# Four kinds of small transfers moved to ScalarE's DMA queue, with a new stage order and new buffer counts, in a hybrid decoder block

## The chip, the cores and the metric

One core of one Trainium2 chip runs the whole kernel. The metric is the device time of one execution in microseconds (us), lower is better; the kernel before is given by the median of three runs. The core has five engines, each of which runs its own list of instructions in order: TensorE (PE in the profile), VectorE (DVE), ScalarE (ACT), GpSimd (POOL) and SyncE (SP). An instruction that has to wait holds up everything behind it on its own engine. A DMA is started by an instruction on an engine's list (here on SP's, and after the change on ACT's too) and carried out by 16 DMA engines.

## The reference

The reference is one decoder layer over 2048 tokens of width 1024, in float32: two groups of heads side by side (gated DeltaNet and retention), an output projection, and a gated MLP with a causal convolution. Cut to what matters:

```python
n    = rms_norm(x, attn_norm_w)                       # (2048, 1024)
proj = n @ w_in                                       # q,k,v,gate,a,b | q,k,v,gate
# gated DeltaNet group: 4 heads of 128; q,k,v = silu(causal conv of width 4)
g    = -exp(a_log) * softplus(a + dt_bias);  beta = sigmoid(b)
gcum = cumsum(g, inside a chunk);  decay = exp(where(causal, gcum_i - gcum_j, -inf))
m    = where(strict, (k * beta) @ k.T * decay, 0)
T    = inverse(eye + m)                               # unit lower triangular
u_base, w_mat, qk = T @ (v * beta), T @ (k * beta * exp(gcum)), (q @ k.T) * decay
for each chunk:                                       # carries state (128 x 128) per head
    u     = u_base - w_mat @ state
    o     = (q * exp(gcum)) @ state + qk @ u
    state = state * exp(gcum_last) + (k * exp(gcum_last - gcum)).T @ u
o_gdn = rms(o) * norm_w * silu(gate)
# retention group: 4 heads of 128, rotary on q,k, fixed decay gamma per head
for each chunk:
    o = ((q @ k.T) * d_mat) @ v + (q * xi) @ r;   r = r * gamma**C + (k * zeta).T @ v
o_ret = silu(gate) * rms(o)
h  = x + concat(o_gdn, o_ret) @ w_out
gg, uu = split(causal_conv_width3(rms_norm(h, mlp_norm_w) @ w_up))   # 2 x 2816
out = rms_norm(h + (silu(gg) * uu) @ w_down, final_norm_w)
```

## The kernel before

**Three stages.** The mixers (up to about 1207 us of the span) run over 4 blocks of 512 tokens, `b = 0..3`. Then `mlp_up` makes the two MLP inputs (to about 2090 us), and `mlp_down` the output. Almost all the work is matmuls on PE. A float32 product is made of three matmuls on float32r halves (high by high, high by low, low by high): L111 to L113 where weights are the stationary side, L383 to L385 where the tokens are. The kernel uses a Strassen-like scheme of 7 products for the output projection and the MLP, whose adds run on DVE.

**Stages of a block.** Each token of `ORDER` is a block number and a stage name. `pro` is the first norm; `k0`, `q0`, `kq`, `v0` are the retention projections (`tok` matmuls). `dec` is `decays`: from the decay inputs it makes the decay sums `gps` (two small matmuls, L460 and L461), transposes them (`gct`, L475) and writes them to device memory as `gdr` (L479). `a0`..`a3` are four steps of one DeltaNet head: `dmat` (L481 to L491) reads `gdr` back as a broadcast to all 128 partitions into `D` (L485) and takes its exponential on ACT (L491); `gdn_kq` and `gdn_v` make q, k, v (`chm` matmuls, convolution, transposes) and the triangular matrix `N`; `gdn_z` (L580 to L587) writes the four diagonal 32-blocks of `N` to `z1` in device memory, by four DMAs. `b0`, `b1` are `gdn_base` for two heads at a time: it reads `z1` back and inverts the 32-blocks on POOL (L600 to L607).

**The recurrence.** `g0`, `g1` are the two pairs of DeltaNet heads: first `gdn_lvls` builds the full inverse from its blocks (`yps`, `ttps`), then four steps of `gdn_rec`, one for each chunk of 128 tokens. One step is a chain that goes back and forth between PE and DVE: `ks` (L679, state times q and k) on PE, a subtraction on DVE (L682), `wps` (L690) on PE, a scaling on DVE (L694), `sps` (L698) on PE, the state's update on DVE (L700), and from there the next step's `ks`. I call each way from PE over DVE back to PE a link; a step has three.

**The rest of a block.** `h0`..`h3` are retention heads (`ret_head`): `rr` (L778), transposes `rtr` (L788), `rkk` (L794), and `ro` (L801 and L802). `p0`, `p1` are the gates. `G0`, `G1` transpose the gated outputs (`mxt`, L420). `W1`..`W7` are the products of the output projection (`wo`, with the split of its input on ACT at L872). `N` is `norm2`: it transposes the normalized rows (`nps`, L907) and writes them to device memory as `n2d` (L909), where `mlp_up` reads them.

**What sets the order.** `ORDER` fixes in which order the stages are handed to the framework. The framework then schedules by a simulation of the engines, with `ORDER` as the priority, and writes a fixed list for each engine. So a token's place moves its instructions, but other stages' instructions come between them. `BUFS` and constants like `NUU` (the buffers of the split inputs in `mlp_down`) set how many buffers each name has, and with that how far one stage may run ahead of another. All DMAs are on SP, so that a DMA that waits for its data holds up all loads behind it.

Of the kernel before, what the change touches and what calls it, by code (L numbers as in the profile page):

```python
# [15 lines left out]
NW = 5  # L16
LA = 1
NHH = 3
NUU = 8
NVR = 4  # L20
NVV = 20
NWUR = 2
# [11 lines left out]
NLATE = 4  # L34
NXR = 7
FD = 4
BUFS = {"n1": 8, "ykq": 5, "kv": 5, "NT": 5, "AT": 5, "o": 2, "n2s": 10, "xk": 2, "og": 1, "co": 7, "Cw": 4,
        "wx": 1, "wsq": 3, "wvr": 3, "wvt": 7, "ca": 8, "mix": 6, "D": 8, "rk": 5, "rq": 4, "rv": 7, "Ar": 1,
        "Nb": 6, "rot": 1, "rrow": 7}

ORDER = ("0pro 0k0 0v0 0dec 0a0 0q0 0a1 0h1 0a2 0b0 0h0 0a3 0b1 0g0 0kq 0p1 0p0 0h3 0h2 0g1 1pro 1k0 0G0 "
# [5 lines left out]
P = 128  # L47
S = 2048
D = 1024
# [3 lines left out]
NT = TB // P  # L53
# [13 lines left out]
def unit(pool, tag, shape, dt=F32, **kw):  # L67

    n = int(np.prod(shape[1:]))
    t = pool.tile([P, U1], dt, tag=tag, name=tag, **kw)[:, :n]  # L70
    if len(shape) == 3:
        t = t.rearrange("p (a b) -> p a b", a=shape[1])
    elif len(shape) == 4:
        t = t.rearrange("p (a b c) -> p a b c", a=shape[1], b=shape[2])
    return t
# [3 lines left out]
def hybrid_block(ctx, tc, x, xT, w_kq, w_v, w_g, w_rk, w_r0, w_r, w_o, w_u, w_d, cols, rows, fnr, masks, rot, out):  # L79
# [47 lines left out]
    seq = []  # L127
    for name in ORDER.split():
        seq += [(None, None, None)] if name == "U" else items[int(name[0])][name[1:]]
# [73 lines left out]
def mixers(ctx, tc, base, base_used, marks, drp, mm3, gamma, mhalf, n1w, n2w, gcw, gv127, epsr, gnw, n2d, hd,  # L203
           x, xT, w_kq, w_v, w_g, w_rk, w_r0, w_r, w_o, rows, masks, rot):
    nc = tc.nc
# [93 lines left out]
    def al(tag, shape, dt=F32):  # L299
        return unit(ap_, tag, shape, dt, **({"bufs": BUFS[tag]} if tag in BUFS else {}))  # L300

    def half(owner, key, tag, i):

        if key not in owner:
            owner[key] = al(tag, [P, 2, TB])
        return owner[key][:, i]
# [32 lines left out]
    def A_items(b, st):  # L339
# [90 lines left out]
        def decays(_):  # L430
            ab = st["ab"]
            a = ab[:, :, 0]
# [43 lines left out]
            gt = small("gt", P, 1)[:16]  # L476
            DVE.tensor_copy(gt, ps[:16, :P])
            gd_ = st["gdr"] = drp.tile([NH, NT, P], F32, tag="gdr", name="gdr")
            nc.sync.dma_start(gd_.rearrange("h c b -> (h c) b"), gt)  # L479

        def dmat(h):  # L481
            def f(_):
                gc = st["gc"]
                Dm = st["D", h] = half(st, ("Dp", h // 2), "D", h % 2).rearrange("p (a b) -> p a b", a=NT)
                nc.sync.dma_start(Dm.rearrange("p a b -> p (a b)"),  # L485
                                  st["gdr"][h].rearrange("a b -> (a b)").partition_broadcast(P))
                for c in range(NT):
                    j = c * NH + h
                    DVE.scalar_tensor_tensor(Dm[:, c, :], Dm[:, c, :], gc[:, j:j + 1], below,
                                             op0=ALU.subtract, op1=ALU.min)  # L490
                ACT.activation(Dm, Dm, AF.Exp)  # L491
            return f
# [83 lines left out]
        v4 = lambda t: t.rearrange("p (c d) -> p c d", d=P)  # L576
# [3 lines left out]
        def gdn_z(h):  # L580
            def f(_):
                if ("z1", h // 2) not in st:
                    st["z1", h // 2] = drp.tile([2, NT, 4, 32, 32], F32, tag="z1", name="z1")
                z1 = st["z1", h // 2][h % 2]
                for k in range(4):
                    sl = slice(k * 32, (k + 1) * 32)
                    nc.sync.dma_start(z1[:, k].rearrange("c j i -> j c i"), v4(st["hd", h]["N"])[sl, :, sl])  # L587
            return f


# [251 lines left out]
    def W_items(b):  # L842
# [19 lines left out]
        def product(i):  # L862
            def f(_):
                vs = [load_v(tc, ap_, w_o, i, k, {"vr": ("wvr", BUFS["wvr"]), "vt": ("wvt", BUFS["wvt"]), "v": ("wv", NWV)},
                             wvc, drp) for k in range(NH)]
# [34 lines left out]
        def norm2(_):  # L900
            for kk in range(4):
                ns = al("n2s", [P, 2, TB])
                for i in range(2):
                    k = 2 * kk + i
                    ps = mbank("nps")
                    for m in range(NT):
                        PE.transpose(ps[:, m * P:(m + 1) * P], C[m][:, k * P:(k + 1) * P], ident)  # L907
                    ACT.activation(ns[:, i], ps, AF.Copy, scale=n2w[:, k:k + 1])
                marks["n", b, kk] = nc.sync.dma_start(n2d[b, kk].rearrange("k p t -> p k t"), ns)  # L909
        return {f"W{i}": [(None, None, product(i))] for i in ORD_DN} | {"N": [(None, None, norm2)]}  # L910

    sts = [dict() for _ in range(NB)]
# [185 lines left out]
def mlp_down(ctx, tc, marks, mm3, sfa, mhalf, hd, aud, w_d, fnr, out):  # L1098
# [15 lines left out]
    def load_u(i, tp):  # L1114
# [8 lines left out]
        for c in range(2):  # L1123
            us.append(unit(wq, "uu", [P, 8, P], F32R, bufs=NUU))
        u3 = unit(wq, "u3", [P, 2, NP - 8, P], F32R, bufs=2)
# [153 lines left out]
```

## Time and profile before

| | before |
|---|---|
| median of 3 runs | 2513.75 us (2513.45 to 2514.49) |
| the profiled execution's own time | 2519.11 us |
| its span in the trace | 2517.3 us |
| VectorE (DVE) busy | 1627.8 us, 65% of the span |
| ScalarE (ACT) busy | 1000.4 us, 40% |
| GpSimd (POOL) busy | 581.7 us, 23% |

The trace is of one execution; its own time is 1.8 us longer than its span. "Busy" leaves out the time an engine takes to start DMAs. In the views, a row `A <- B` says that the engine's instruction A was idle until instruction B on another engine was done.

### The profile page before, as it was taken

The page shows a single profiled execution, that of the slowest core. Times are in us where ns is not written, and L with a number is a line of the kernel's source. Part 1 is how long each engine was busy: PE and PEld are TensorE (multiplying, and loading weights), DVE is VectorE, ACT ScalarE, POOL GpSimd, SP SyncE. Part 2 cuts the span into 40 slices and gives each one's busy share as a digit, 9 for nine tenths or more (in the row PEclk, how much of TensorE's full clock was granted, in tenths as well). Part 3 has the DMA queues.
Part 4 walks back from the last instruction along what each step waited for, and adds up shares of the span by engine and source line. Part 5 has one row for each costly group of instructions (what it writes and reads, how often), then busy time and mean ns, then how long its engine had stood idle before and what let it go on. Part 6 is the DMA issues. An engine that isn't in the chain of part 4 may idle for free.

```text
span 2517.3 us, 35733 instructions
## 1 busy us (share of the span) xinstructions
PE 2430.2 (97%) x12476; PEld 2036.1 (81%) x12476; DVE 1627.8 (65%) x3198; ACT 1000.4 (40%) x2150; POOL 581.7 (23%) x891
## 2 busy tenths in 40 slices
PE   8999799999999989998899999999999999999998
PEld 7877688787888878887688888888888888888887
DVE  5755677435652663445889898897565567555795
ACT  6634445434433542324454443442222224433332
POOL 1355136531064205150011000000000001422180
PEclk9999799999999999999999999999999999999999
DMA  8756388863685646652889877867676868764794
GB/s 320 245 190 218 115 319 318 306 222 136 229 285 161 212 159 212 247 186 85 319 340 351 316 296 286 306 254 273 241 251 224 285 240 283 221 211 152 240 300 135
DMA packets 285604, 609.64 MB, mean 242 GB/s; under 512 B 40880, under 2 KB 120944, under 8 KB 285424
## 3 DMA queue, kind: packets, MB, share of 16 engines
q1 hardware_dynamic: 285424, 607.36, 68.7%
q8 instruction: 98, 1.61, 0.3%
q14 instruction: 82, 0.67, 0.1%
HBM read 410.56 MB, written 196.71 MB: 241 GB/s over the span
## 4 chain that ended last, share of the span: by engine, by line
PE 79%; POOL 7%; DVE 6%; DMA 3%; ACT 3%; issue 2%; SPq 0%; POOLq 0%; DVEq 0%; ACTq 0%
PE p L111 10%; PE p L112 10%; PE p L113 10%; PE tok L383 5%; PE tok L385 5%; PE tok L384 5%; PE d L113 5%; PE d L112 5%; PE d L111 5%; POOL pers L605 2%; POOL pers L603 2%; PE chm L111 2%; PE chm L113 2%; PE chm L112 2%; PE wo L111 2%
## 5 line engine op out<-in xcount | busy, mean ns | idle before, releaser
L111 PE MATMUL p<-x,wu 128*128 128x512 f32 x1176 | 454.6, 391 | 6.2 <-ACT x L928 5.8
L112 PE MATMUL p<-x,wu 128*128 128x512 f32 x1176 | 458.5, 390 | 1.9 <-DVE x L929 1.9
L113 PE MATMUL p<-x,wu 128*128 128x512 f32 x1176 | 451.5, 390 | 0.0
L383 PE MATMUL tok<-wc,n 128*128 128x512 f32 (+2 forms) x768 | 274.0, 363 | 13.0 <-ACT n L371 9.6
L384 PE MATMUL tok<-wc,n 128*128 128x512 f32 (+2 forms) x768 | 276.1, 360 | 0.0
L385 PE MATMUL tok<-wc,n 128*128 128x512 f32 (+2 forms) x768 | 275.8, 362 | 0.0
L111 PEld LDWEIGHTS p<-x,wu 128*128 128x128 f32 x1176 | 221.2, 188 | 54.6 <-ACT x L928 8.3
L112 PEld LDWEIGHTS p<-x,wu 128*128 128x128 f32 x1176 | 221.0, 188 | 48.9 <-DVE x L929 3.2
L113 PEld LDWEIGHTS p<-x,wu 128*128 128x128 f32 x1176 | 221.0, 188 | 45.8
L1049 DVE SCALAR_TENSOR_TENSOR acc<-uc,base,acc 128x1023 f32<-128x1023 f32 (+1 forms) x176 | 221.3, 1280 | 41.3 <-ACT acc L1046 39.8
L1007 DVE TENSOR_TENSOR uc<-p,uc 128x512 f32<-128x512 f32 x224 | 153.6, 689 | 138.0 <-PE p L113 137.4
L177 POOL TENSOR_TENSOR vt<-vr 128x512 f32<-128x512 f32 x44 | 70.0, 1596 | 618.4 <-DMA au<-acc 422.9
L112 PE MATMUL d<-v,uu 128*128 128x512 f32 x448 | 174.3, 389 | 0.0
L111 PE MATMUL d<-v,uu 128*128 128x512 f32 x448 | 174.3, 389 | 0.0
L113 PE MATMUL d<-v,uu 128*128 128x512 f32 x448 | 174.3, 389 | 0.0
L383 PEld LDWEIGHTS tok<-wc,n 128*128 128x128 f32 x768 | 146.2, 191 | 32.8 <-ACT n L371 9.6
L384 PEld LDWEIGHTS tok<-wc,n 128*128 128x128 f32 x768 | 146.4, 191 | 19.6
L385 PEld LDWEIGHTS tok<-wc,n 128*128 128x128 f32 x768 | 145.4, 190 | 20.0
L111 PE MATMUL chm<-n,wc 128*128 128x512 f32 x384 | 152.9, 398 | 0.0
L113 PE MATMUL chm<-n,wc 128*128 128x512 f32 x384 | 152.2, 396 | 0.0
L112 PE MATMUL chm<-n,wc 128*128 128x512 f32 x384 | 152.0, 396 | 0.0
L1054 POOL COPY base<-uc 128x2 f32<-128x2 f32 x44 | 35.2, 799 | 454.4 <-DVE uc L1007 453.6
(247 smaller groups left out, 4897.0 us busy)
## 6 DMA issues: line engine op xcount, KB each, us to landing
wu<-wu SPq DMA_DIRECT2D x308, 512.0 KB, 6.0
wc<-wd SPq DMA_DIRECT2D x166, 512.0 KB, 5.5
wv<-wo SPq DMA_DIRECT2D x84, 512.0 KB, 5.9
wd<-wc SPq DMA_DIRECT2D x60, 512.0 KB, 5.1
ur<-au SPq DMA_DIRECT2D x56, 512.0 KB, 5.8
wur<-in_w_u SPq DMA_DIRECT2D x44, 512.0 KB, 6.1
au<-st SPq DMA_DIRECT2D x88, 256.0 KB, 4.6
vr<-in_w_d SPq DMA_DIRECT2D x44, 512.0 KB, 6.0
```

The source lines that it names most:

```text
L111: PE.matmul(ps, ah, bh, start=(first and i == 0), stop=False, skip_group_check=chk)
L112: PE.matmul(ps, ah, bl, start=False, stop=False, skip_group_check=chk)
L113: PE.matmul(ps, al, bh, start=False, stop=(i == n - 1), skip_group_check=chk)
L177: POOL.tensor_tensor(tt[:, j], a, b_, op=ALU.subtract)
L383: PE.matmul(ps, ah, wh, start=(k == 0), stop=False)
L384: PE.matmul(ps, ah, wl, start=False, stop=False)
L385: PE.matmul(ps, al_, wh, start=False, stop=(k == KT - 1))
L603: POOL.tensor_tensor(tm[:, :, :n], Nb[:, j:j + 1, j + 1:].to_broadcast([P, 8, n]), X[:, :, j:j + 1].to_broadcast([P, 8, n]), op=ALU.mult)
L605: POOL.tensor_tensor(X[:, :, j + 1:], X[:, :, j + 1:], tm[:, :, :n], op=ALU.add)
L1007: add = lambda o, ps, a: DVE.tensor_tensor(o, ps, a, op=ALU.add)
L1049: DVE.scalar_tensor_tensor(acc[:, t:], u[:, :T2 - t], w, acc[:, t:], op0=ALU.mult, op1=ALU.add)
L1054: POOL.tensor_copy(mhalo[:, ci], u[:, T2 - 2:])
```

## The change

Four lines change the engine that starts a DMA from SP to ACT: the write of the decay sums `gdr` (L479, 4 DMAs in the program), their broadcast to `D` (L485, 16), the blocks of the triangular matrices to `z1` (L587, 64) and the normalized rows to `n2d` (L909, 16), 100 DMAs together. The reads of `z1` and `n2d` stay on SP. Seven buffer counts change by one or two, and `ORDER` is rewritten in places.

```diff
@@ -16,7 +16,7 @@
 NW = 5
 LA = 1
 NHH = 3
-NUU = 8
+NUU = 10
 NVR = 4
 NVV = 20
 NWUR = 2
@@ -34,15 +34,15 @@
 NLATE = 4
 NXR = 7
 FD = 4
-BUFS = {"n1": 8, "ykq": 5, "kv": 5, "NT": 5, "AT": 5, "o": 2, "n2s": 10, "xk": 2, "og": 1, "co": 7, "Cw": 4,
-        "wx": 1, "wsq": 3, "wvr": 3, "wvt": 7, "ca": 8, "mix": 6, "D": 8, "rk": 5, "rq": 4, "rv": 7, "Ar": 1,
+BUFS = {"n1": 8, "ykq": 5, "kv": 4, "NT": 5, "AT": 6, "o": 2, "n2s": 11, "xk": 2, "og": 1, "co": 6, "Cw": 4,
+        "wx": 1, "wsq": 3, "wvr": 3, "wvt": 8, "ca": 8, "mix": 6, "D": 8, "rk": 5, "rq": 4, "rv": 8, "Ar": 1,
         "Nb": 6, "rot": 1, "rrow": 7}
 
-ORDER = ("0pro 0k0 0v0 0dec 0a0 0q0 0a1 0h1 0a2 0b0 0h0 0a3 0b1 0g0 0kq 0p1 0p0 0h3 0h2 0g1 1pro 1k0 0G0 "
-         "1dec 0G1 0W1 0W2 1q0 0W6 1a0 0W7 1a1 0W5 1a3 1v0 0W3 1h1 1b0 0W4 1a2 1h0 0N 1kq 1b1 1g0 2pro "
-         "1p0 1p1 1h2 1g1 1h3 2k0 1G0 1G1 2v0 2dec 1W1 1W2 2a0 1W6 2a1 1W7 1W5 1W3 2a2 2b0 2q0 1W4 2h1 "
-         "2a3 2b1 2h0 2g0 2g1 1N 3pro 2p1 2p0 2kq 2h2 2G0 3k0 2h3 2G1 3dec 2W1 2W2 3a1 3a0 2W6 3v0 3b0 "
-         "3q0 3h1 2W7 2W5 2W3 3h0 3a3 3p0 3a2 3b1 3g0 3kq 3h2 3h3 2W4 3g1 3G0 2N 3p1 3G1 3W1 3W2 3W6 3W7 "
+ORDER = ("0pro 0k0 0v0 0dec 0a0 0q0 0a1 0a2 0h0 0b0 0h1 0a3 0b1 0g0 0kq 0g1 0h2 0p1 1pro 0p0 1k0 0G0 0h3 "
+         "1dec 0G1 0W1 1a0 0W2 1q0 0W6 0W7 1a1 0W5 1a3 1v0 0W3 1h1 1b0 0W4 1a2 1h0 0N 1kq 1b1 1g0 2pro "
+         "1p1 1h2 1p0 1g1 1h3 2k0 1G0 1G1 2v0 2dec 1W1 1W2 2a0 1W6 1W7 1W5 1W3 2a2 2a1 2b0 2q0 1W4 2h1 "
+         "2a3 2b1 2h0 2g0 2g1 1N 3pro 2p1 2kq 2h2 2p0 2G0 3k0 2h3 2G1 3dec 3a0 2W1 2W2 3a1 2W6 3v0 3b0 "
+         "3q0 3h1 2W7 2W5 3a2 2W3 3h0 3a3 3b1 3kq 3p0 3g0 3h2 2W4 3g1 3G0 2N 3p1 3h3 3G1 3W1 3W2 3W6 3W7 "
          "3W5 3W3 3W4 3N")
 P = 128
 S = 2048
@@ -476,13 +476,13 @@
             gt = small("gt", P, 1)[:16]
             DVE.tensor_copy(gt, ps[:16, :P])
             gd_ = st["gdr"] = drp.tile([NH, NT, P], F32, tag="gdr", name="gdr")
-            nc.sync.dma_start(gd_.rearrange("h c b -> (h c) b"), gt)
+            nc.scalar.dma_start(gd_.rearrange("h c b -> (h c) b"), gt)
 
         def dmat(h):
             def f(_):
                 gc = st["gc"]
                 Dm = st["D", h] = half(st, ("Dp", h // 2), "D", h % 2).rearrange("p (a b) -> p a b", a=NT)
-                nc.sync.dma_start(Dm.rearrange("p a b -> p (a b)"),
+                nc.scalar.dma_start(Dm.rearrange("p a b -> p (a b)"),
                                   st["gdr"][h].rearrange("a b -> (a b)").partition_broadcast(P))
                 for c in range(NT):
                     j = c * NH + h
@@ -584,7 +584,7 @@
                 z1 = st["z1", h // 2][h % 2]
                 for k in range(4):
                     sl = slice(k * 32, (k + 1) * 32)
-                    nc.sync.dma_start(z1[:, k].rearrange("c j i -> j c i"), v4(st["hd", h]["N"])[sl, :, sl])
+                    nc.scalar.dma_start(z1[:, k].rearrange("c j i -> j c i"), v4(st["hd", h]["N"])[sl, :, sl])
             return f
 
 
@@ -906,7 +906,7 @@
                     for m in range(NT):
                         PE.transpose(ps[:, m * P:(m + 1) * P], C[m][:, k * P:(k + 1) * P], ident)
                     ACT.activation(ns[:, i], ps, AF.Copy, scale=n2w[:, k:k + 1])
-                marks["n", b, kk] = nc.sync.dma_start(n2d[b, kk].rearrange("k p t -> p k t"), ns)
+                marks["n", b, kk] = nc.scalar.dma_start(n2d[b, kk].rearrange("k p t -> p k t"), ns)
         return {f"W{i}": [(None, None, product(i))] for i in ORD_DN} | {"N": [(None, None, norm2)]}
 
     sts = [dict() for _ in range(NB)]
```

What the framework's schedule makes of it is shown at three places. The first is PE's list at the end of block 0, where block 1's decay sums (`gps`, `gct`) stand among the last steps of the second pair's recurrence. Before:

```order
L460 MATMUL gps<-pers_230,base 128x16
L461 MATMUL gps<-pers_230,pers_118 128x16
L679 MATMUL ks<-pers_125,ykq 128x128 x4
L475 MATMUL gct<-base,pers_230 16x128
L690 MATMUL wps<-kv,AT 128x128 x2
L698 MATMUL sps<-pers_1355,kv 128x128 x2
L698 MATMUL sps<-pers_1355,AT 128x128 x2
L679 MATMUL ks<-pers_125,ykq 128x128 x4
L690 MATMUL wps<-kv,AT 128x128 x2
L698 MATMUL sps<-pers_1355,kv 128x128 x2
L698 MATMUL sps<-pers_1355,AT 128x128 x2
L420 MATMUL mxt<-base,mix 128x128 x16
```

After the change it reads:

```order
L794 MATMUL rkk<-ykq 128x128 x4
L460 MATMUL gps<-pers_230,base 128x16
L461 MATMUL gps<-pers_230,pers_118 128x16
L698 MATMUL sps<-pers_1355,kv 128x128 x2
L698 MATMUL sps<-pers_1355,AT 128x128 x2
L475 MATMUL gct<-base,pers_230 16x128
L679 MATMUL ks<-pers_125,ykq 128x128 x4
L690 MATMUL wps<-kv,AT 128x128 x2
L698 MATMUL sps<-pers_1355,kv 128x128 x2
L698 MATMUL sps<-pers_1355,AT 128x128 x2
L778 MATMUL rr<-rv,rk 128x128 x4
L801 MATMUL ro<-rv,Ar 128x128
```

Before, the pair's third and fourth steps (`ks`, `wps`, `sps` each) stand behind the sums with nothing but the sums between, and 16 transposes `mxt` of `G0` follow. Now only the third step's `sps` and the fourth step stand there. The first and second step have moved up, among projections, transposes and `rrp`, and behind the recurrence stand the `rr` and `ro` of two retention heads, between which `G0`'s last `mxt` come.

The second place is ACT's list at the same point of the program; `D` is the exponential's tile, and L685 and L705 belong to the recurrence. Before:

```order
L705 ACTIVATE pers_601<-o 128x128
L469 ACT_TABLE_LOAD
L469 ACTIVATE pers_230<-pers_230 128x32
L705 ACTIVATE pers_601<-o 128x128
L471 ACTIVATE pers_230<-pers_230 128x16
L685 ACTIVATE o<-ks,pers_230 128x128 x2
L705 ACTIVATE pers_601<-o 128x128 x2
L491 ACTIVATE D<-D 128x512
L685 ACTIVATE o<-ks,pers_230 128x128 x2
L491 ACTIVATE D<-D 128x512 x3
```

After the change:

```order
L479 DMA gdr<-pers_230 16x128
L685 ACTIVATE o<-ks,pers_230 128x128 x2
L485 DMA D<-gdr 128x512
L423 ACTIVATE og<-mxt,base 128x256
L485 DMA D<-gdr 128x512 x2
L705 ACTIVATE pers_601<-o 128x128
L485 DMA D<-gdr 128x512
L705 ACTIVATE pers_601<-o 128x128
L491 ACTIVATE D<-D 128x512 x3
L804 ACTIVATE o<-ro 128x512
```

The write of `gdr` and the four reads of `D` are now instructions of ACT, between L685 and L705 of the recurrence, with the exponentials (L491) behind them.

The third place is PE's list at the end of block 2, in the last steps of its second pair. Before:

```order
L698 MATMUL sps<-pers_1355,kv 128x128 x2
L698 MATMUL sps<-pers_1355,AT 128x128 x2
L794 MATMUL rkk<-ykq 128x128 x4
L679 MATMUL ks<-pers_125,ykq 128x128 x4
L690 MATMUL wps<-kv,AT 128x128 x2
L698 MATMUL sps<-pers_1355,kv 128x128 x2
L698 MATMUL sps<-pers_1355,AT 128x128 x2
L679 MATMUL ks<-pers_125,ykq 128x128 x4
L690 MATMUL wps<-kv,AT 128x128 x2
L698 MATMUL sps<-pers_1355,kv 128x128 x2
L698 MATMUL sps<-pers_1355,AT 128x128 x2
L778 MATMUL rr<-rv,rk 128x128 x4
```

After the change:

```order
L679 MATMUL ks<-pers_125,ykq 128x128 x4
L111 MATMUL chm<-n_8272,wc 128x512
L112 MATMUL chm<-n_8272,wc 128x512
L113 MATMUL chm<-n_8272,wc 128x512
L690 MATMUL wps<-kv,AT 128x128 x2
L698 MATMUL sps<-pers_1355,kv 128x128 x2
L698 MATMUL sps<-pers_1355,AT 128x128 x2
L679 MATMUL ks<-pers_125,ykq 128x128 x4
L690 MATMUL wps<-kv,AT 128x128 x2
L698 MATMUL sps<-pers_1355,kv 128x128 x2
L698 MATMUL sps<-pers_1355,AT 128x128 x2
L778 MATMUL rr<-rv,rk 128x128 x4
```

Block 3's first head (`3a0`, whose `chm` matmuls have 512 columns) has moved up: three of them stand between `ks` and `wps` of the third step, and the 42 rows ahead of the ones shown, on both sides of the second step's `sps`, are `chm` too. The retention head's `rkk` stands earlier now; the fourth step and the `rr` behind it are as before.

## The prediction

> **What bounds the kernel.** I read the page's busy times first, then PE's waits, then windows and the timeline around them.
>
> ```profile
> span 2517.3 us, 35733 instructions
> PE 2430.2 (97%) x12476; PEld 2036.1 (81%) x12476; DVE 1627.8 (65%) x3198; ACT 1000.4 (40%) x2150; POOL 581.7 (23%) x891
> ```
>
> PE is busy for 97% and its list of matmuls is the same work after the change. So only two things can be gained on PE: its idle time, 2517.3 - 2430.2 = 87 us, and the matmuls that ran at half the clock. Which waits make the idle time (us in total, times, longest):
>
> ```profile
> PE tok L383 <- ACT n L371: 9.6, 1, 9.6
> PE mxt L420 <- DVE mix L418: 9.4, 4, 4.2
> PE sps L698 <- DVE pers L694: 8.1, 12, 2.4
> PE wo L111 <- ACT wu L872: 8.0, 5, 2.2
> PE wps L690 <- DVE kv L682: 7.1, 11, 2.1
> PE ks L679 <- DVE pers L700: 5.3, 9, 1.5
> PE ro L801 <- DVE Ar L795: 3.8, 1, 3.8
> PE wo L111 <- ACT wv L197: 3.7, 1, 3.7
> PE tok L383 <- DMA wc<-wd: 1.1, 1, 1.1
> PE ro L802 <- DVE pers L780: 0.9, 2, 0.7
> ```
>
> The first is the start, which the change leaves. The three rows of the recurrence (sps, wps, ks) make 20.5 us, the gates' mxt 9.4. For loads PE waited 1.1 us in all. Where they lie, by stretches (from and to, length, PE busy and instructions, granted clock, DMA share, GB/s):
>
> ```profile
> 150.50:166.00 15.50, 10.66 (x49) 0.78 0.12 35
> 214.00:233.00 19.00, 13.39 (x66) 0.82 0.12 30
> 264.00:314.00 50.00, 33.20 (x178) 0.66 0.15 49
> 606.00:635.00 29.00, 22.93 (x143) 0.94 0.29 101
> 877.00:918.00 41.00, 32.08 (x178) 0.88 0.28 91
> ...
> 1250.00:2454.00 1204.00, 1202.29 (x5316) 1.00 0.77 267
> ...
> 279.10:313.20 34.10, 21.94 (x82) 0.50 0.11 32
> 1187.10:1197.30 10.20, 7.68 (x26) 0.50 0.47 151
> ```
>
> The MLP is full: 1.7 us idle in 1204, so more buffers there (`NUU`) can give at most that, and I take 0. The ends of blocks 0, 2 and 3 hold what there is. They are where a recurrence runs bare: a link waits for DVE, the wait lowers the clock, and at the low clock the next matmuls take twice as long.
>
> **The order, place by place.** The worst is the end of block 0:
>
> ```profile
> 267.64 1.12 PE L658 MATMUL ttps<-AT,pers 128*64 128x64 f32 x16 [0.57 <-issue]
> 270.27 0.46 PE L690 MATMUL wps<-kv,AT 128*128 128x128 f32 x2 [1.52 <-issue]
> 276.84 0.49 PE L679 MATMUL ks<-pers,ykq 128*128 128x128 f32 x2 [1.52 <-DVE pers L700]
> 285.01 2.06 PE L679 MATMUL ks<-pers,ykq 128*128 128x128 f32 x8
> 292.02 2.07 PE L679 MATMUL ks<-pers,ykq 128*128 128x128 f32 x8 [0.44 <-DVE pers L700]
> 304.52 3.65 PE L420 MATMUL mxt<-base,mix 128*128 128x128 f32 x16 [4.17 <-DVE mix L418]
> ...
> 256.88 1.16 PE L778 MATMUL rr<-rv,rk 128*128 128x128 f32 x8
> ```
>
> From ks to ks, 285.01 to 292.02, a bare step takes 7.0 us at half clock. In block 2 the same step at full clock is:
>
> ```profile
> 881.68 1.06 PE L679 MATMUL ks<-pers,ykq 128*128 128x128 f32 x8
> 883.18 0.75 PE L690 MATMUL wps<-kv,AT 128*128 128x128 f32 x4 [0.45 <-DVE kv L682]
> 884.46 0.68 PE L698 MATMUL sps<-pers,kv 128*128 128x128 f32 x4 [0.53 <-DVE pers L694]
> 886.03 1.19 PE L679 MATMUL ks<-pers,ykq 128*128 128x128 f32 x8 [0.44 <-DVE pers L700]
> ```
>
> It takes 4.35 us, of which 0.45 + 0.53 + 0.44 are waits, so 2.9 are work. One step more now stands among other matmuls: 7.0 - 2.9 = 4.1 us gained. The levels and the first step, with waits of 0.57, 1.52 and 1.52, have moved up among projections: 3.6 gained. At the end two retention heads come in. Each has an rr of 1.16 and a ro of twice as many matmuls, about 1.8 at the rr's pace: 3.0 at full clock and 6.0 at half: two cost 6.0 more where the clock is low, and cover the 4.17 for mix: 1.8 lost. **Block 0's end: -4.1 - 3.6 + 1.8 = -5.9, taken as -6.** Bounds: +6 if nothing but the heads' low clock comes; -13 if the clock is up in what is left (the 21.94 us at half would be 11, and two thirds of the bare part remain: 7 more).
>
> 214 to 233 is the first pair's recurrence, 5.6 us idle (19.00 - 13.39) and 6.8 us at half clock (the clock's missing 0.18 of 19, twice). Of its four bare links two now have other matmuls between: I take half of 5.6 + 3.4, rounded down, **-4**, between 0 and -9. 150 to 166: the retention head that waited 3.8 us for Ar has moved; its wait and the clock's loss after it, 0.22 of 15.5 or 3.4 us, may go or come back at the new place: **-2**, between -7 and +4. At 877 to 918, block 3's first head takes away four of nine bare links at 0.44 to 0.54: **-2**, between -7 (the clock too, 0.12 of 41 us) and +5 (the head's later matmuls are missing as cover elsewhere). At block 3's end the last retention head now stands ahead of the transposes that waited 4.07 us for mix:
>
> ```profile
> 1188.17 3.67 PE L420 MATMUL mxt<-base,mix 128*128 128x128 f32 x16 [4.07 <-DVE mix L418]
> 625.71 2.17 PE L420 MATMUL mxt<-base,mix 128*128 128x128 f32 x12 [0.50 <-DVE mix L418]
> ```
>
> In block 1, where such a head already stands there, the wait is 0.50. I take the 2.9 us of the head's rr and ro: **-2.9**, between -9 (the 10.2 us at half clock too) and +3 (the head is at half clock). Against that, two more heads have nothing between rr and ro, at 0.7 each by the longest row of ro L802: **+1.3**. The fewer `kv` buffers and the other counts I take at 0: they act through the order already built. Their cover is the projections between two blocks; without it, the longest wait for kv, 2.1 us, at three block changes: +6.
>
> **The queue.** What moves, by line (ns min/median/max of one, first and last start):
>
> ```profile
> L587 SPq DMA_DIRECT2D z<-NT x64: 303/423/1226, 76.8 to 1089.9; - x64
> L485 SPq DMA_DIRECT2D D<-gdr x16: 319/423/1260, 53.5 to 913.2; - x16
> ...
> SPq L587 <- DVE AT L556: 83.7, 16, 10.0
> SPq L479 <- DVE pers L477: 54.4, 4, 18.1
> SPq L909 <- ACT n2s L908: 49.9, 11, 30.2
> ...
> gdr<-pers SPq DMA_DIRECT2D x4, 8.0 KB, 1.4
> ...
> 0.00:1200.00 1200.00, 518.32 (x1431) 0.97 0.62 219
> ```
>
> SP loses 100 issues, 42 us at the rows' median of 0.42 (80 stand in them, the other 20 taken alike), and the waits of 83.7, 54.4 and 49.9, 188 us. But PE waited 1.1 us for loads, so this gives nothing on PE; 1.1 is its bound. ACT (last row: its busy time in the mixers, 518 of 1200 us) gets the 42 us of issues. Behind each stand the instructions that PE or the recurrence wait for: the recurrence's o (L685, L705), the splits wu (L872), the conversions of wv (L197). PE waits for these in two rows above, wu 8.0 and wv 3.7; 42 on 518 is 8%, 1 us of them. And each block's D reads wait on ACT until gdr has landed, 1.4 us, with o and the exponentials behind: with the three reads' issues ahead of the last, 0.42 each, that is 2.7 us for a block; four blocks, a quarter of it felt by PE, 2.7: **+4** in all. Bounds: 0 (ACT is idle more than half the time) and +24, in the second rival. The Trainium skill, "DMA: Bandwidth & Descriptors", section "Issuing engines are not separate DMA queues", says that transfers started by several engines run on the same 16 DMA engines and that only the issuing time is saved. The trace has more to be saved on SP, the 188 us of waiting in order beside the 42; by either the sum stays, as PE does not wait for SP.
>
> **The sum:** -6 - 4 - 2 - 2 - 2.9 + 1.3 + 4 = -11.6 us against the profiled execution's 2519.11 (span 2517.3 and 1.8 around it): 2507.5. That execution was 5.4 us over the median of 2513.75, so the forecast for a median is 2513.75 - 11.6, about 2502.
>
> **Rivals.** *Only the place of the waits moves.* What covers a link now uncovers another: block 3's end gains a head that the block's middle loses, and the clock stays low because the covers are short 128-wide matmuls and transposes. For it speaks the row at 1187.10: 7.68 us busy of 10.20, 3.67 of it transposes (row 1188.17), and the clock at 0.50 throughout. Against it: at 606 to 635 a block's end with retention heads ran at 0.94. The gain is then the 4 at 214 less the queue's 4, and the block 0 and block 3 terms shrink to about 2: 2512. The Trainium skill, "TensorE: Matmul & The Clock Gate", part 1 and part 4, has the clock follow PE's activity in windows of about 3.4 us, and says that transposes don't count as busy the way matmuls do; the row at 1187.10 agrees. By that page block 0's end would keep its low clock, and the sum would lean to this rival.
>
> *ACT is held up (slower).* The moved DMAs stand in 24 groups (16 heads' z1, 4 blocks' gdr and D, 4 of n2d). SP waited 83.7 us in 16 times for AT, 5.2 each; if ACT arrives too early even by a part of that, the splits, o and exponentials behind it are late, and PE with them. At 1.0 us on PE for a group it costs 24 against the order's -15.6: 2513.75 + 8.4 = 2522. It breaks even at 15.6 / 24 = 0.65 us a group. For it: most PE waits in the bare links are already without slack. Against it: the schedule puts each DMA on ACT near the time its data should be there, and ACT is idle for 57% of the mixers.
>
> *The queue part does nothing.* SP's freed 230 us meet no wait of PE, and ACT's idle time takes all the issues. The order alone gives -15.6: 2498.
>
> **Chances.** The forecast (2502) 0.46; the queue for nothing (2498) 0.10; only the place moves (2512) 0.22; ACT held up (2522) 0.22. A measurement of this kernel can tell about 0.2%, 5 us, from no change. The first two are faster by more than that, 0.56; the third within, 0.22; the fourth slower, 0.22. The range takes in the first three and the fourth's near end: below, block 0's clock up (7 more) and the queue's 4 for nothing, 2502 - 11 = 2491; above, 2522.
>
> **What would show it.** Right: 264 to 314's counterpart shorter by about 6 us, the longest mxt wait under 2 us in blocks 0 and 3, PE's idle near 77 us, SP's waits for AT, pers and n2s gone. Wrong on the queue: PE's waits for wu and wv well above their 11.7 us, or new ones for o, or ACT's own queue waiting for AT for more than some 20 us with PE idle beside it. Wrong on the order: new waits of sps, wps and ks, or new stretches at half clock, where 0h1, 3a0 and 3h3 were taken away. The forecast falls if the clock, not the waits, decides: then half-clock time, not idle time, will differ.

## The result, and the profile after

| | before | after |
|---|---|---|
| median of 4 runs beside each other | 2514.12 us (2513.45 to 2518.28) | 2494.61 us (2491.82 to 2497.46) |
| ratio, 95% interval | | 0.9919 (0.9902 to 0.9936) |
| profiled execution, own time and span | 2519.11, 2517.3 us | 2495.60, 2493.8 us |
| PE idle (span less busy) | 87.1 us | 80.6 us |

The kernel is 0.8% faster, about 20 us. The forecast was 2502 (2491 to 2522), a gain of 11.6. The first lines of the changed kernel's page, and the longest of its waits of PE in the mixers (total, times, longest; left-out rows are marked by dots):

```profile
span 2493.8 us, 35729 instructions
PE 2413.2 (97%) x12476; PEld 2019.8 (81%) x12476; DVE 1622.6 (65%) x3198; ACT 1000.8 (40%) x2151; POOL 574.4 (23%) x891
...
PE wo L111 <- ACT wv L197: 6.3, 3, 4.5
PE wo L111 <- ACT wu L872: 6.0, 4, 1.6
PE sps L698 <- DVE pers L694: 5.8, 11, 0.7
PE wps L690 <- DVE kv L682: 5.8, 11, 1.0
...
PE ks L679 <- ACT mix L396: 5.7, 1, 5.7
...
PE ro L802 <- DVE pers L780: 3.4, 3, 1.7
...
PE mxt L420 <- DVE mix L418: 2.8, 4, 1.4
PE ks L679 <- DVE pers L700: 2.6, 6, 0.6
```

Against the rows of before, the recurrence's three links (sps, wps, ks behind DVE) went from 20.5 to 14.2 us, and their longest waits from 2.4, 2.1 and 1.5 to 0.7, 1.0 and 0.6; mxt went from 9.4 to 2.8. A new wait of 5.7 us for the gates' mix on ACT came in, and the waits for wv grew from 3.7 to 6.3. In all, PE's idle time is only 6.5 us less. But the span is 23.5 us less. The other 17 us are PE's busy time, which fell from 2430.2 to 2413.2 for the same matmuls. That is the clock. The windows over all stretches that were granted half the clock (the tail left out), of before (the first of nine, and the sum; the longest, 34.10 us, is in the prediction) and then of after (from and to, length, PE busy, granted clock, DMA share, GB/s):

```profile
152.80:159.60 6.80, 5.26 (x20) 0.50 0.16 36
...
sum 81.70, PE 62.19; mean PE 6.91
```

```profile
214.70:221.50 6.80, 3.23 (x12) 0.50 0.09 24
269.30:279.50 10.20, 8.99 (x39) 0.50 0.06 19
286.40:289.80 3.40, 3.40 (x15) 0.50 0.00 0
436.60:443.40 6.80, 5.45 (x13) 0.50 0.73 244
617.50:620.90 3.40, 3.40 (x13) 0.50 0.68 245
sum 30.60, PE 24.48; mean PE 4.90
```

Work at half clock takes about twice its time (eight `ks` matmuls took 2.06 us at 285.01 and 1.06 us at 881.68, in the prediction's rows), so half of "PE busy" in these stretches is lost: 62.19 / 2 = 31.1 us before, 24.48 / 2 = 12.2 after, 18.9 less. Every span here is three parts: PE's work at full clock (busy less the lost part: 2399 before, 2401 after), PE's idle time, and the lost clock. 87.1 to 80.6 and 31.1 to 12.2 make -25.4; with 2 us more of work that is the spans' -23.5.

Where it went, by stretches, before and then after:

```profile
12.00:190.00 178.00, 172.11 (x997) 0.98 0.68 248
190.00:250.00 60.00, 54.39 (x293) 0.94 0.61 217
250.00:330.00 80.00, 63.20 (x459) 0.79 0.41 149
330.00:500.00 170.00, 164.97 (x810) 0.99 0.89 320
800.00:950.00 150.00, 140.00 (x880) 0.97 0.50 173
1100.00:1250.00 150.00, 132.32 (x786) 0.94 0.55 195
```

```profile
12.00:190.00 178.00, 174.54 (x1023) 1.00 0.69 249
190.00:250.00 60.00, 53.60 (x393) 0.94 0.71 259
250.00:330.00 80.00, 70.28 (x415) 0.91 0.60 212
330.00:500.00 170.00, 161.09 (x867) 0.98 0.85 297
800.00:950.00 150.00, 143.48 (x924) 1.00 0.56 194
1100.00:1250.00 150.00, 130.92 (x785) 1.00 0.60 215
```

Length less busy is idle; the lost clock is worked out as above from the half-clock stretches inside. 250 to 330, block 0's end, gained most: idle 16.8 to 9.7, lost clock 11.0 to 6.2.

**How far one profile goes.** An execution's lost clock varies. Over the 17 to 19 executions of the kernel before that were taken beside each of the three sets of experiments, its time ran from 2508 to 2522 us. Every execution has its mean granted clock, and (1 - clock) x 2 x span is its time at half clock, which broadly goes with the time: 71 us on average before, 36 in the four executions after. By the two sums above a microsecond at half clock loses 0.38 to 0.40 (31.1 of 81.70, 12.2 of 30.60), so the 35 us less are some 14 of the 20. The profiled execution of before, with 81.7 us, was a long one.

### The profile page after: what moved, and what is told of

It is laid out like the page before. It is cut to its first block, busy times and chain, and to the rows that moved or that the text cites. A ratio compares the mean times of both kernels' runs of the same rounds, so it can differ in the third digit from the quotient of the medians.

```text
span 2493.8 us, 35729 instructions
## 1 busy us (share of the span) xinstructions
PE 2413.2 (97%) x12476; PEld 2019.8 (81%) x12476; DVE 1622.6 (65%) x3198; ACT 1000.8 (40%) x2151; POOL 574.4 (23%) x891
## 4 chain that ended last, share of the span: by engine, by line
PE 78%; POOL 6%; DMA 6%; DVE 5%; issue 3%; ACT 2%; SPq 0%; ACTq 0%; POOLq 0%; DVEq 0%
PE p L111 10%; PE p L112 10%; PE p L113 10%; PE d L113 5%; PE d L111 4%; PE d L112 4%; PE tok L383 4%; PE tok L385 4%; PE tok L384 4%; PE chm L111 2%; PE chm L113 2%; PE chm L112 2%; POOL pers L605 2%; POOL pers L603 2%; DMA wvr<-in_w_o 2%
## 5 line engine op out<-in xcount | busy, mean ns | idle before, releaser
L383 PE MATMUL tok<-wc,n 128*128 128x512 f32 (+2 forms) x768 | 274.8, 362 | 10.8 <-ACT n L371 10.2
L1049 DVE SCALAR_TENSOR_TENSOR acc<-uc,base,acc 128x1022 f32<-128x1022 f32 (+1 forms) x176 | 221.2, 1279 | 40.0 <-ACT acc L1046 34.3
L383 PEld LDWEIGHTS tok<-wc,n 128*128 128x128 f32 x768 | 145.9, 190 | 30.4 <-ACT n L371 10.2
```

Source lines behind the costliest of these rows:

```text
L383: PE.matmul(ps, ah, wh, start=(k == 0), stop=False)
L1049: DVE.scalar_tensor_tensor(acc[:, t:], u[:, :T2 - t], w, acc[:, t:], op0=ALU.mult, op1=ALU.add)
```

## The experiments

Twelve kernels ran. "Half clock" is the mean of the executions; "idle" and "lost" are of the one profile (lost: half of PE's busy time at half clock).

| kernel | median us | ratio to before (95%) | half clock | idle | lost |
|---|---|---|---|---|---|
| before | 2514 to 2516 | 1 | 71 | 87.1 | 31 |
| after | 2494.6 | 0.9919 (0.9902-0.9936) | 36 | 80.6 | 12 |
| e1 order and buffers | 2500.1 | 0.9933 (0.9916-0.9949) | 46 | 77.3 | 17 |
| e2 queue | 2506.1 | 0.9959 (0.9944-0.9974) | 59 | 85.8 | 19 |
| e3 block 0's order | 2516.7 | 0.9996 (0.9983-1.0009) | 67 | 84.1 | 26 |
| e4 buffers | 2515.0 | 1.0007 (0.9995-1.0018) | 71 | 86.4 | 23 |
| e5 before, filled links | 2519.9 | 1.0025 (1.0015-1.0035) | 60 | 91.6 | 23 |
| e6 after, filled links | 2501.3 | 0.9948 (0.9931-0.9964) | 35 | 74.2 | 15 |
| e7 after, n2d on SP | 2492.7 | 0.9915 (0.9900-0.9930) | 35 | 75.7 | 12 |
| e8 rest of the order | 2512.2 | 0.9989 (0.9980-0.9999) | 55 | 86.8 | 22 |
| e9 after, gdr and D on SP | 2497.6 | 0.9928 (0.9913-0.9943) | 36 | 79.4 | 12 |
| e10 after, z1 on SP | 2509.7 | 0.9976 (0.9964-0.9989) | 46 | 82.3 | 18 |
| e11 after, rest of the order old | 2502.8 | 0.9944 (0.9929-0.9959) | 45 | 82.0 | 19 |
| e12 after, block 0's order old | 2512.0 | 0.9990 (0.9980-1.0000) | 57 | 92.3 | 17 |

(e6's half clock is of three executions. The fourth was recorded with a clock of 0.942 at 2502.04 us, a time that the others reached with 0.992 to 0.994.)

### e1: order and buffers without the queue

```diff
-            nc.scalar.dma_start(gd_.rearrange("h c b -> (h c) b"), gt)
+            nc.sync.dma_start(gd_.rearrange("h c b -> (h c) b"), gt)
```

The same at the other three places (D, z1, n2d); `ORDER`, `BUFS` and `NUU` are the changed kernel's.

> The changed kernel's order and buffer counts, with all 100 transfers back on SyncE's queue. Theory order (the gain is work standing in the recurrence's links, above all at the end of block 0, where PE then keeps its full clock): 2491 to 2500 us, nearly the whole 19.5 us of gain, half-clock stretches before the tail below 40 us in all. Theory queue (the gain is SyncE freed of 188 us of waiting in order): 2508 to 2514. Theory pair (the order needs the queue): 2500 to 2508. Rival slow queue (the transfers on ScalarE cost 4 us and more): below 2491.

2500.1 us, 0.9933. About 16 of the 20 us are there without the queue. The windows at block 0's end in this kernel:

```profile
250.00:330.00 80.00, 68.41 (x409) 0.94 0.60 218
```

Idle is 11.6 instead of 16.8, at a clock of 0.94 instead of 0.79. The time lies on the boundary between "order" and "pair", and the half-clock stretches before the tail are 41.0 us in the profile, where "order" asked for under 40: "queue" is ruled out, "order" only just holds. The intervals of e1 and of the changed kernel overlap, so what the queue adds to this order, some 5 us by the medians, is not measured clear of noise.

### e2: the queue without the order

```diff
-                    nc.sync.dma_start(z1[:, k].rearrange("c j i -> j c i"), v4(st["hd", h]["N"])[sl, :, sl])
+                    nc.scalar.dma_start(z1[:, k].rearrange("c j i -> j c i"), v4(st["hd", h]["N"])[sl, :, sl])
```

The same at the other three places, on the kernel before.

> The kernel before with the four kinds of transfers on ScalarE's queue and nothing else changed; block 0's end keeps its bare links in PE's list. Theory order: 2512 to 2519 us (the forecast's +4 for ScalarE's issues, or nothing), the 34 us at half clock at the end of block 0 stay. Theory queue: 2495 to 2502. Theory pair: 2508 to 2514.

2506.1 us, 0.9959: a gain of 10 that "order" does not have, though less than "queue" asked for; it lies in none of the three ranges. 16 and 10 make 26, the two together 20. And PE's list is not that of before: when the transfers changed engines, the schedule moved rows in it (548 lines of difference, names' numbers left out). So e2 tests the queue and another order at once. PE's idle time is 85.8, nearly as before; what fell is the lost clock.

### e3 and e8: the two parts of the order alone

e3 takes `ORDER` of the changed kernel up to block 1's `1dec` on the kernel before, e8 what is behind it. The first lines of e3:

```diff
-ORDER = ("0pro 0k0 0v0 0dec 0a0 0q0 0a1 0h1 0a2 0b0 0h0 0a3 0b1 0g0 0kq 0p1 0p0 0h3 0h2 0g1 1pro 1k0 0G0 "
...
+ORDER = ("0pro 0k0 0v0 0dec 0a0 0q0 0a1 0a2 0h0 0b0 0h1 0a3 0b1 0g0 0kq 0g1 0h2 0p1 1pro 0p0 1k0 0G0 "
+         "0h3 1dec 0G1 0W1 0W2 1q0 0W6 1a0 0W7 1a1 0W5 1a3 1v0 0W3 1h1 1b0 0W4 1a2 1h0 0N 1kq 1b1 "
...
```

> The kernel before with only the first part of ORDER new, up to block 1's decay sums; buffers and queues are as before. Theory order, with the end of block 0 as its main place: 2496 to 2503 us, that is 11 to 18 of the 19.5. If the gain is spread over the blocks as the forecast had it (block 0's three terms made 12 of 16.8): 2501 to 2505. Theory queue: 2513.

> The kernel before with ORDER new only from block 1's decay sums on; block 0's part, buffers and queues as before. After e1 (order and buffers: -16) and e3 (block 0's part alone: 0) the order's gain should be here if parts add up: 2497 to 2503. If the parts need each other, or the queue: 2508 to 2515.

2516.7 (0.9996) and 2512.2 (0.9989): nothing and 2.6 us. e3 is no change, which of its three theories only "queue" had; e8 lies where it was put if the parts need each other or the queue. The parts do not add up to e1's 16. In e3 PE's list at block 0's end has the new pattern (one bare step fewer, two heads behind it), but block 0's end gained only half of what it gained in e1: idle 14.3 and 7.5 lost, against 11.6 and 4.0. A wait of 2.81 us for kv was left there that neither e1 nor the changed kernel has. e11, below, does not have it either, though the order behind block 0 is the old one there too. What e1, e11 and the changed kernel share and e3 lacks is the buffer counts. Which of the counts removes it was not found.

### e4: the buffer counts alone

```diff
-NUU = 8
+NUU = 10
-BUFS = {"n1": 8, "ykq": 5, "kv": 5, "NT": 5, "AT": 5, "o": 2, "n2s": 10, "xk": 2, "og": 1, "co": 7, "Cw": 4,
+BUFS = {"n1": 8, "ykq": 5, "kv": 4, "NT": 5, "AT": 6, "o": 2, "n2s": 11, "xk": 2, "og": 1, "co": 6, "Cw": 4,
...
```

> The kernel before with only the seven buffer counts changed; PE's list at the end of block 0 is almost that of before. All theories that I hold: 2512 to 2516 us, no difference. If the counts carry the gain (more wvt, rv and split inputs let loads and splits run further ahead): below 2505.

2515.0, 1.0007: by themselves nothing, as forecast.

### e5 and e6: filling the short waits

Does a short wait cost by bringing the half clock? In both kernels two matmuls were put into a step, into a part of `wps`'s bank that nobody reads: in e5 in the second pair's steps 2 to 4 of block 0 of the kernel before, in e6 in those of all blocks of the changed kernel.

```diff
-                ps = rbank("wps")
-                us = []
+                ps, us = rbank("wps"), []
+                fil = lambda: (b == 0 and hs[0] == 2 and c > 0) and PE.matmul(ps[:, 2 * P:], H[0]["ykq"][:, 0, sl], H[0]["ykq"][:, 1, :2 * P], start=True, stop=True); fil()
                 for i, e in enumerate(H):
-                    PE.matmul(ps[:, i * P:(i + 1) * P], e["TT"][:, sl], e["vp"][:, sl], start=True, stop=True)
+                    PE.matmul(ps[:, i * P:(i + 1) * P], e["TT"][:, sl], e["vp"][:, sl], start=True, stop=True); i and fil()
```

> The kernel before with six matmuls more (128x256, their result is not used) in the second pair's bare links of block 0: one between ks and wps and one between wps and sps, in steps 2 to 4. PE gets 3 us more work and nothing useful. Theory clock (the short waits cost little by themselves; what costs is the half clock that they bring): half-clock time at the end of block 0 under 15 us instead of 24 to 34, 2504 to 2511 us. Theory wait (the idle time itself is the cost): 2514 to 2519, no gain.

> The changed kernel with the same six matmuls in the second pair's steps 2 to 4 of all four blocks (24). Theory clock: half-clock time per execution from 36 us to under 28, 2487 to 2493 us. Theory wait: 2495 to 2500, the 24 matmuls' work on top.

2519.9 (1.0025) and 2501.3 (0.9948): both 5 to 7 us slower than without. "Clock" failed in both, and both times lie about 1 us above the range of "wait". In e5 half-clock time did fall, 71 to 60 us, and still it lost. The timeline of PE in e5 shows one reason (start, length, operation, in brackets the idle time before and what ended it):

```profile
288.92 1.06 PE L688 MATMUL wps<-ykq 128*128 128x256 f32 x2
289.77 1.06 PE L690 MATMUL wps<-kv,AT 128*128 128x128 f32 x4
290.63 0.75 PE L688 MATMUL wps<-ykq 128*128 128x256 f32 x2
293.86 0.87 PE L698 MATMUL sps<-pers,kv 128*128 128x128 f32 x4 [2.48 <-DVE pers L694]
```

The step's ks runs up to these rows, and the link from ks to wps has no wait left, but the fill took as long as the wait had. The one that matters is still there, 2.48 us for L694. So a matmul without use fills a short wait at the price of the wait, and does not reach the long one. e6, where PE's list otherwise hardly moved, says the same: idle falls by 6.4, work grows by 9.6, lost clock does not fall. In e5 the schedule also moved rows of PE's list behind the fills (most of them between 300 and 500 us, and again from 900 us on), so not all of its 5 us need be the fills'.

Why the long ones are long can be read from DVE's list. Its timeline at the end of block 0, before and after:

```profile
293.15 1.14 DVE L489 SCALAR_TENSOR_TENSOR D<-D,pers,base 128x128 f32<-128x128 f32 x4 [0.52 <-DMA D<-gdr]
294.20 0.60 DVE L682 SCALAR_TENSOR_TENSOR kv<-ks,pers,kv 128x128 f32<-128x128 f32 x2
294.72 3.23 DVE L489 SCALAR_TENSOR_TENSOR D<-D,pers,base 128x128 f32<-128x128 f32 x12
297.87 0.61 DVE L694 TENSOR_SCALAR pers<-wps,pers 128x128 f32<-128x128 f32 x2
```

```profile
275.83 0.61 DVE L694 TENSOR_SCALAR pers<-wps,pers 128x128 f32<-128x128 f32 x2 [0.79 <-PE wps L690]
...
278.35 0.61 DVE L700 SCALAR_TENSOR_TENSOR pers<-pers,pers,sps 128x128 f32<-128x128 f32 x2 [0.86 <-PE sps L698]
...
280.65 1.14 DVE L489 SCALAR_TENSOR_TENSOR D<-D,pers,base 128x128 f32<-128x128 f32 x4
...
281.98 2.19 DVE L489 SCALAR_TENSOR_TENSOR D<-D,pers,base 128x128 f32<-128x128 f32 x8
...
284.28 1.14 DVE L489 SCALAR_TENSOR_TENSOR D<-D,pers,base 128x128 f32<-128x128 f32 x4
```

Before, 3.23 us of block 1's subtractions on `D` stood between the pair's L682 and L694, and PE waited 2.38 us for L694. After, all sixteen stand behind the pair's last L700, where the two retention heads give PE work.

### e7, e9, e10: one kind of transfer back on SyncE

Each is the changed kernel with one kind back: n2d (16), gdr and D (20), z1 (64).

```diff
-                marks["n", b, kk] = nc.scalar.dma_start(n2d[b, kk].rearrange("k p t -> p k t"), ns)
+                marks["n", b, kk] = nc.sync.dma_start(n2d[b, kk].rearrange("k p t -> p k t"), ns)
```

> The changed kernel with the 16 writes of n2d back on SyncE's queue; the lists of PE, DVE and POOL are instruction for instruction those of the changed kernel. Theory order: 2492 to 2498, no difference. If ScalarE's issue of these writes costs (16 x 0.4 us and what stands behind): 2 to 6 us faster. If SyncE's waits for them hold up loads: 2498 to 2505.

> The changed kernel with the decay sums' write and the 16 broadcasts of D back on SyncE's queue (20 transfers). PE's list is that of the changed kernel through the end of block 0 and beyond, apart from two swaps of neighbours; later 128 rows have moved. Theory lists (the queue counts only by what the schedule makes of it): 2491 to 2498, block 0's end as in the changed kernel. Theory SyncE (its waiting for the sums in order costs PE): 2498 to 2504, with the loss at block 0's end. If ScalarE's issues of these cost: 2487 to 2491.

> The changed kernel with the 64 writes of z1 back on SyncE's queue; the schedule moves some 600 rows of PE's list by it. If the whole step from e1 (2500) to the changed kernel (2494.6) hangs on z1: 2498 to 2503. If on none of the three kinds by itself: 2492 to 2497. ScalarE's issues cost: below 2491.

2492.7, 2497.6 and 2509.7 us. e7 is the clean one, with the same lists on PE, DVE and POOL; e9 has nearly the same list on PE (128 lines of difference, two of the moves up to the end of block 0). Their intervals overlap the changed kernel's, though SyncE waits again: "order" held in e7, and "lists" in e9 by 0.4 us. SyncE's waits in e7 and in e9:

```profile
SPq L909 <- ACT n2s L908: 58.1, 11, 41.4
```

```profile
SPq L479 <- DVE pers L477: 45.9, 4, 15.1
```

58 and 46 us of waiting in order on SyncE, and ScalarE relieved of 16 or 20 issues, change nothing that can be measured. e10 lies above all its ranges: it is slower by 15 us, with 608 lines of difference in PE's list, and slower even than e1, which has z1 and the other three kinds on SyncE. So there is no price for z1 on a queue that adds up; with lists that differ, its direct share could not be separated. No one place carries the 15 us: the profile's sums are 2 us of idle, 6 of lost clock and 3 of work above the changed kernel's, spread over 12 to 250 us and the MLP's start and what follows it, and that profile lies 4 us under its median.

### e11 and e12: the changed kernel with one half of the order old

```diff
-         "1dec 0G1 0W1 1a0 0W2 1q0 0W6 0W7 1a1 0W5 1a3 1v0 0W3 1h1 1b0 0W4 1a2 1h0 0N 1kq 1b1 1g0 2pro "
...
+         "0h3 1dec 0G1 0W1 0W2 1q0 0W6 1a0 0W7 1a1 0W5 1a3 1v0 0W3 1h1 1b0 0W4 1a2 1h0 0N 1kq 1b1 "
...
```

These are two lines of e11, which has the order behind `1dec` as before; e12 has that up to `1dec` as before.

> The changed kernel (queue, buffers, block 0's new order) with ORDER from block 1's decay sums on as before. If block 0's gain (by the traces some 16 us of idle and lost clock up to 330 us) needs only the queue, the buffers and its own order: 2498 to 2504, and the losses at 800 to 950 and 1100 to 1250 us are those of before. If it needs the order behind it too (block 1's first head ahead of W2): 2505 to 2510.

> The changed kernel with block 0's part of ORDER as before. If the parts add up (queue -9 from e2, the order's rest -3 from e8): 2500 to 2505. If the queue's gain was the same stretch at block 0's end that the new order mends too: 2500 to 2505 as well but with 20 us at half clock at block 0's end; if it is a matter of this very schedule: anything up to 2512.

2502.8 and 2512.0 us. With the queue and the buffers in place, taking back block 0's order costs 17 us, taking back the rest costs 8 (the last two intervals just overlap). In e11 block 0's end keeps its gain (12.9 idle, 1.7 lost), while 800 to 950 and 1100 to 1250 have the losses of before: 10.4 and 4.8 there, and 18.3 and 6.9. In e12 it is the other way round; block 0's end has 17.8 and 5.7, and the long waits are 2.65, 2.52 and 4.17 us, where the kernel before has 2.06, 2.38 and 4.17. e11 came out as expected; e12 had the expected 20 us at half clock at block 0's end, but its time is that of the third case, a matter of this very schedule. So block 0's order is most of the gain here, and nothing by itself (e3).

## Why the prediction was right, and where it was too small

**The place and the direction held.** PE's idle time and clock at the ends of blocks 0, 2 and 3 gave the gain, by the order with the buffer counts (e1, e11, e12); the whole order with the old counts was not run. The terms, in us of idle and lost clock together, by the two traces:

| term | forecast | measured |
|---|---|---|
| block 0's end (250 to 330) | -6 | 27.8 to 15.9, -11.9 |
| first pair (190 to 250) | -4 | 8.4 to 8.0, -0.4 |
| first retention head (12 to 190) | -2 | 8.6 to 3.5, -5.1 |
| block 0's output projection (330 to 500) | 0 | 6.7 to 11.6, +4.9 |
| block 2's end (800 to 950) | -2 | 14.5 to 6.5, -8.0 |
| block 3's end and the MLP's start (1100 to 1250) | -2.9 | 24.5 to 19.1, -5.4 |

These are the two traces' differences, and the trace of before was one of the slower executions; in medians the sum is some 4 us less. The three ends can be followed through all fourteen profiles, as idle time and lost clock together in us:

| place | order that bears on it new | old |
|---|---|---|
| block 0's end (250 to 330) | 11.4 to 15.9 in seven profiles, 21.7 in e3 | 21.1 to 29.1 in six |
| block 2's end (800 to 950) | 5.7 to 8.8 in eight | 9.4 to 15.2 in six |
| block 3's end and the MLP's start (1100 to 1250) | 17.6 to 22.3 in eight | 23.8 to 25.2 in six |

Block 0's gain is there in every profile that has its new order and the new buffer counts, with the queue or without; e3 alone has the order without the counts. The gains of blocks 2 and 3 go with the second half of the order alone: e8 has them without counts and queue. But e8 gained only 2.6 us in its median, so not all of this reaches the total; where it goes is open.

**The clock decided, and the size inside the range is partly luck.** The prediction's own last sign was that the forecast falls if the clock, not the waits, decides, and that then half-clock time will differ. So it came: idle time fell by 6.5 us, to 80.6 where about 77 was forecast, and the lost clock by 18.9; by the executions' means the clock is some 14 of the 20. The range's lower end, 2491, was worked out for block 0's clock coming up and a queue that costs nothing, and both came true. But the other terms were off by up to 6 us each, in both directions, and that they nearly cancel is luck.

**The mis-sized term is the clock at block 0's end.** The forecast took the step that went, 4.1 us, and the first waits, 3.6, and then charged the two heads 6 us for a clock that it thought would stay low; its lower bound of -13 was the case with the clock up. The clock came up: 0.79 to 0.91 in that stretch, the half-clock time in it 34.1 to 13.6 us. Blocks 2 and 3 were mis-sized by the same: the waits gave 3.5 us at block 2's end and took 1.4 at block 3's, the lost clock gave 4.5 and 6.8. Block 2's clock part may be chance: e2, e4 and e5 lost none there with that part of the order old. Block 3's is not: the six profiles with the old order lost 5.1 to 6.9 us there, the other eight 0 to 4.8.

**The cover was argued from the wrong side.** The forecast counted links without PE work in them. The runs showed that filling a bare link of about 0.5 us costs at least what it saves (e5, e6), and that at full clock such links left the clock alone (last section). What went are longer waits: 2.06 and 2.38 us for a DVE that was busy with other work (rotations and gates, then `D`; PE waits 2.06 us for L682 at 280.76 and 2.38 for L694 at 298.27), and 4.17 for the last mix, which two heads now cover. That DVE's list explains the first two is read from the traces; no run moved that work alone.

**The first pair was wrong.** Its four waits of 0.70 to 1.42 us, and one of 1.29 for the gates' mix behind them, became one of 5.70 for that mix and one of 0.70; with the lost clock the sum is nearly the same.

**The heads' rr and ro:** +1.3 was forecast, by the traces the waits of ro L802 for L780 went from 0.9 to 3.4, +2.5.

**The queue's +4 is not there.** ScalarE took the issues (z1 with a median of 0.44 us) without a measurable loss in e7 and e9, and SyncE's waits for n2s and pers, 104 of its 188 us, were worth nothing there, as the forecast had it. But "the order and the queue are two terms of a sum" was wrong: moving transfers moved the schedule's lists, and e2 and e10 differ by 10 and 15 us from their neighbours with it. The rule of the Trainium skill ("DMA: Bandwidth & Descriptors", "Issuing engines are not separate DMA queues") that only the issuing time is saved agrees with e7 and e9, the two with nearly equal lists.

**The rivals.** ACT held up was to show as larger waits for wu and wv: 11.7 went to 12.3 us. "Only the place moves" described the first pair (190 to 250) and block 0's output projection (330 to 500), and not the block ends. What the prediction took for it from the Trainium skill ("TensorE: Matmul & The Clock Gate", part 4), that transposes do not count as busy the way matmuls do, these traces do not bear out: in e2 the transposes `mxt` filled the stretch from 297.59 to 301.01 at half clock by themselves, and the clock came back behind it.

```profile
297.42 3.68 PE L420 MATMUL mxt<-base,mix 128*128 128x128 f32 x16 [4.08 <-DVE mix L418]
...
297.59:301.01 3.42, 3.42 (x16) 0.50 0.00 0
301.01:304.42 3.41, 1.96 (x9) 1.00 0.00 0
```

The low clock at 1187.10 needs no such rule: a wait of 4.07 us ended at 1188.17 and one of 1.45 us stood behind the transposes, and by the shares in the last section such gaps are enough. "The queue does nothing" agrees with e7 and e9 for n2d and for gdr and D by themselves, and is open for z1.

No version clearly beat the changed kernel. e7 is 2 us under it, within both intervals.

## What to carry to other kernels

Split a span into PE's work at full clock, its idle time and the time lost at half clock before any term is sized: here the idle time moved by 6.5 us and the clock by 19. Look for the few waits over a microsecond and for what the other engine was doing instead, and do not fill short waits in a chain with work that nobody needs. A clock that has fallen can stay low through such waits, so take away what makes it fall. Where a scheduler sets the order, no edit is alone: compare the engines' lists before taking two runs for a test of one cause.

## What the runs showed of the hardware that was not expected

**Short waits did not lower a full clock, but a low clock stayed low through them.** In the changed kernel at block 3's end the waits from 1128 to 1159 us, twelve of 0.41 to 0.54 us each, left the clock at 1.00; PE was busy for 34 of 40 us there. The first and the last of the twelve in the timeline, and the window:

```profile
1128.07 0.75 PE L690 MATMUL wps<-kv,AT 128*128 128x128 f32 x4 [0.44 <-DVE kv L682]
...
1158.32 0.75 PE L698 MATMUL sps<-pers,kv 128*128 128x128 f32 x4 [0.44 <-DVE pers L694]
...
1120.00:1160.00 40.00, 34.25 (x271) 1.00 0.23 79
```

In the kernel before, at block 0's end, waits of 0.44 and 0.57 us stood in a stretch that was already at half clock, and it stayed there. PE was busy for 2.53 and 2.84 of 3.41 us in the two rows below; in the changed kernel 2.34 of 3.41 (1129.49 to 1132.90) kept the full clock.

```profile
285.97:289.38 3.41, 2.53 (x11) 0.50 0.01 2
289.38:292.79 3.41, 2.84 (x11) 0.50 0.54 135
```

**The same wait may or may not cost a low clock.** The retention head's 3.80 us wait of before was followed by 6.8 us at half clock, the changed kernel's wait of 3.46 at the same place by none, and in e7, with the same list on PE, a wait of 3.28 by 3.4 us. All stretches at half clock inside the kernels are 3.4 us or a multiple of it (6.8, 10.2, 34.1), and in each of the fourteen traces they start whole multiples of 3.41 us apart. So the clock goes by windows on a fixed grid, and a wait counts by how it falls into them. The changed kernel's wait fell on two windows and left PE busy for 1.68 of 3.41 us in each; the other two waits lay mostly in one window and left 1.11 and 0.22 us. The rows are the changed kernel's wait and its two windows, then the last window ahead of the low clock, first of the kernel before and then of e7:

```profile
151.60 0.46 PE L801 MATMUL ro<-rv,Ar 128*128 128x128 f32 x2 [3.46 <-DVE Ar L795]
...
146.45:149.86 3.41, 1.68 (x10) 1.00 0.12 48
149.86:153.28 3.42, 1.68 (x15) 1.00 0.38 73
...
149.43:152.84 3.41, 1.11 (x5) 1.00 0.51 208
...
149.40:152.81 3.41, 0.22 (x1) 1.00 0.00 0
```

Counted over all fourteen traces (from 12 us to 25 us before the end), every window at full clock in which PE was busy for less than 0.43 of the time was followed by half clock (67 windows), none above 0.61 was, and of 126 between, 37 were. The clock came back only behind half-clock windows with PE busy for 0.82 or more, 104 times; nine as busy as that stayed low, and why is open. The windows are placed differently in the traces of the changed kernel and of e7, which have the same list on PE. This fits the spread of one kernel's executions, 2508 to 2522 us, which goes with their mean clock; no kernel has two traces here that would show it. The Trainium skill ("TensorE: Matmul & The Clock Gate", part 1) has the clock set by windows of about 3.4 us, and the lengths agree.
